# Handing the first token tile from mixer to attention: dealt by transfers and turned by VectorE instead of transposed by TensorE

## The chip, the cores and the metric

The kernel runs on one core of one Trainium2 chip. The metric is the device time of one execution in microseconds (us), as the median of several runs. The engines are TensorE (PE; its weight loads are PEld), VectorE (DVE), ScalarE (ACT), GpSimd (POOL) and SyncE (SP, which here only issues transfers).

## The reference

The model has two layers (DEPTH = 2) on 256 tokens of width 1024, all in float32. Each layer has four steps, and each step ends in a layer norm over the 1024 columns:

```python
h = layer_norm(ALPHA * h + 0.5 * swiglu(h, ffn1...), ln_g[l, 0], ln_b[l, 0])
...   # mixer: z = h @ w_in[l], a gated convolution, a gated recurrence, a multi-scale pooling
h = layer_norm(ALPHA * h + mix, ln_g[l, 1], ln_b[l, 1])          # mix = [...] @ w_out[l]
h = layer_norm(ALPHA * h + cross_attn(h, mem, ca_q[l], ca_k[l], ca_v[l], ca_o[l]), ln_g[l, 2], ln_b[l, 2])
h = layer_norm(ALPHA * h + 0.5 * swiglu(h, ffn2...), ln_g[l, 3], ln_b[l, 3])
```

Cross-attention projects h to queries (ca_q) and a memory of 256 rows to keys and values (ca_k, ca_v), takes a softmax for four heads of width 256, and projects back with ca_o. The change lies between the second and the third line: the norm that ends the mixer, and the way its result reaches the query projection.

## The kernel before, in words

**Split products.** To keep float32 accuracy, every operand of a product is split into a rounded part and a low part (the difference to the rounded part). The helper `split` does it: ScalarE rounds (line 75), VectorE subtracts (line 76). A product is then three matmuls: rounded by rounded, rounded by low, low by rounded (line 132 issues each). Weights arrive through SP's queue in pieces of 128x1024 (`raw`, six places) and are split into `whi` and `wlo` (eight places each). So VectorE and ScalarE work for every weight piece that TensorE uses.

**Tiles of tokens and the transposed copy.** The activation h lies as two tiles of 128 tokens by 1024 columns, `h[0]` and `h[1]`. Products need it with the columns on the partitions: that is `xT`, with the rounded part `xTh` and the low part `xTl`, in eight chunks k of 128 columns. It is made from h by `transposed`: for each half of the chunks four TensorE transposes into PSUM (line 199), then a split.

**The end of a step.** `project_back` multiplies by the output weights in four slabs of two chunks. Its last three slabs are done per token tile inside `finish`: `tile_done(i)` runs the products of tile i for both halves of 512 columns, adds them to h (line 377), takes the statistics of the norm, and applies the norm in two passes (lines 407 and 412). The statistics come in two forms. With `junk` set, line 377 also sums, VectorE forms the mean (line 387), ScalarE squares all 1024 columns with a sum (line 392), VectorE forms the variance (line 398), GpSimd takes the power -1/2 (line 404). Without `junk`, VectorE uses its statistics instruction (line 383), combines them (lines 402 and 403), and GpSimd takes the power. The mixer's end is the one end in a layer that runs without `junk` in this kernel (the kernel's last norm does too). When the products of tile 1 are under way, `turn_first` transposes tile 0; `finish` returns a function, `pend`, that transposes tile 1 later.

**Attention.** `attention` first multiplies memory by the first half of ca_v (`values(l, 0, ...)`, which does not need h), calling `pend` in the middle of the second tile of memory rows, then projects queries (`query(0)`, `query(1)`), four chunks of 128 columns each. For each chunk, `mm_cols` issues seven products of the rounded weights with both parts of `xT`, eight products of the low weights, and the last rounded product. The four softmax heads follow, whose weights are dealt by transfers and turned by VectorE's 32x32 transposes; that pair of steps is a full transpose of the tile. Query weights are loaded behind the mixer's last norm pass (`normed[-1]`) as far as VectorE's queue is concerned, through `tc.issue_after`.

**What sets the order.** The order of each engine's instructions is fixed when the program is built. A scheduler plays the program against estimated durations; among the instructions that are ready it takes the one earliest in program order, and what isn't ready is passed by others. `tc.issue_after(x)` queues the instructions of a block behind x on x's engine. Some stretches of the mixer have an order written out by hand; the handover to attention has none. On the chip each engine then keeps that order and waits on semaphores.

Of the kernel before, what the change touches and what calls it, by code (L numbers as in the profile page):

```python
# [60 lines left out]
def model(ctx: ExitStack, tc: tile.TileContext, t: dict, out: bass.AP):  # L61
# [7 lines left out]
        return ps.tile(list(shape), F32, tag=tag, name=tag)  # L69


    loads, normed, squared, halfway, lows, turns = [], [], [], [], [], []

    def split(hi, lo, src):
        rounded = nc.scalar.copy(hi, src)  # L75
# [117 lines left out]
    kTh = cst.tile([P, NK, SEQ], F32R, name="kTh")  # L193
    kTl = cst.tile([P, NK, SEQ], F32R, name="kTl")

    def transposed_half(src, i, j, dh, dl, unit=idn, keep=None):
        pt = acc((P, 4, P))
        for k in range(4):
            turns.append(nc.tensor.transpose(pt[:, k, :], src[:, (4 * j + k) * P : (4 * j + k + 1) * P], unit))  # L199
        split(dh[:, 4 * j : 4 * j + 4, tok(i)], dl[:, 4 * j : 4 * j + 4, tok(i)], pt)  # L200
        if keep:
            nc.scalar.copy(keep[j], pt)

    def transposed(src, i, dh, dl, unit=idn, keep=None):
        for j in range(2):
            transposed_half(src, i, j, dh, dl, unit, keep)
            if not j:
                halfway.append(lows[-1])

# [115 lines left out]

    squares = kTh[:, 4:8, :].rearrange("p k c -> p (k c)")

    def finish(mm, y, scale, gb, units, last=False, junk=None, ahead=None, prompt=False):

        g, b = gb
        def later_split(i, j, unit):
            pt = acc((P, 4, P))
            for k in range(4):
                turns.append(nc.tensor.transpose(pt[:, k, :], h[i][:, (4 * j + k) * P : (4 * j + k + 1) * P], unit))
            dh, dl = (x[:, 4 * j : 4 * j + 4, tok(i)] for x in (xTh, xTl))
            nc.scalar.copy(dh, pt)  # L340
            return dh, dl, pt

        def turn_first():
            if prompt:
                held.extend(later_split(0, j, units[0]) for j in range(2))
            else:
                transposed(h[0], 0, xTh, xTl, units[0])

        def low_part(w):
            lows.append(nc.vector.tensor_tensor(w[1], w[2], w[0].bitcast(F32), op=ALU.subtract))  # L350

        held = []

        def tile_done(i):

            st = sm.tile([P, 4, 6], F32, tag="st", name="st")
            pieces, size = [slice(0, 512), slice(512, DM)], 512
            if last and i == NT - 1:

                pieces, size = [slice(0, 512), slice(512, 768), slice(768, DM)], 256  # L360
                c = slice(512, DM)
                v = halves(h[i][:, c])
                with tc.issue_after(lows[-1].ins):
                    nc.vector.scalar_tensor_tensor(v, v, ALPHA / scale, sums(y[i][1]), op0=ALU.mult, op1=ALU.add)
            for c in pieces:
                n = c.start // 512
                v = halves(h[i][:, c])
                if len(pieces) == 3 and n:
                    o = acc((P, 256))
                    mm(i, n, slice(c.start - 512, c.stop - 512), o, None)  # L370
                    nc.vector.tensor_tensor(v, v, sums(o), op=ALU.add)
                else:
                    mm(
                        i, n, slice(0, 512), None,
                        None if last or not i or not n else turn_first,
                    )
                    nc.vector.scalar_tensor_tensor(
                        v, v, ALPHA / scale, sums(y[i][n]), op0=ALU.mult, op1=ALU.add,
                        accum_out=None if junk is None else st[:, n, 0:1],
                    )  # L380
                for d in range(c.start, c.stop, size):
                    if junk is None:
                        nc.vector.bn_stats(st[:, d // size, :], h[i][:, d : d + size])
            mv = sm.tile([P, 2], F32, tag="mv", name="mv")
            rs = sm.tile([P, 1], F32, tag="rs", name="rs")
            if junk is not None:
                mean = nc.vector.tensor_scalar(
                    mv[:, 0:1], st[:, 0, 0:1], st[:, 1, 0:1], -1.0 / DM, op0=ALU.add, op1=ALU.mult
                )
                with ExitStack() as behind:  # L390
                    squared.append(
                        nc.scalar.activation(junk, h[i], AF.Square, bias=mv[:, 0:1], accum_out=mv[:, 1:2])
                    )
                    if prompt:
                        with tc.issue_after(mean.ins):
                            low_part(held.pop(0))
                        behind.enter_context(tc.issue_after(lows[-1].ins))
                    nc.vector.tensor_scalar(
                        rs, mv[:, 1:2], 1.0 / DM, LN_EPS / scale / scale, op0=ALU.mult, op1=ALU.add
                    )  # L400
            else:
                nc.vector.bn_aggr(mv, st[:, 0 : DM // size, :])
                nc.vector.tensor_scalar_add(rs, mv[:, 1:2], LN_EPS / scale / scale)
            nc.gpsimd.tensor_tensor(rs, rs, nhalf[:, 0:1], op=ALU.pow)
            cs = [slice(0, 512), slice(512, DM)]
            for c in cs:
                nc.vector.scalar_tensor_tensor(
                    h[i][:, c], h[i][:, c], mv[:, 0:1], g[:, c],
                    op0=ALU.subtract if junk is None else ALU.add, op1=ALU.mult,
                )  # L410
            for c in pieces:
                normed.append(nc.vector.scalar_tensor_tensor(
                    h[i][:, c], h[i][:, c], rs, b[:, c], op0=ALU.mult, op1=ALU.add
                ))
                if last:
                    e = nc.scalar if c.start == 512 else nc.sync
                    e.dma_start(out[0, tok(i), c], h[i][:, c])

        if ahead is None:
            tile_done(0)  # L420
            tile_done(1)
        else:
            split(*ahead.todo[0])
            if prompt:
                nc.scalar.copy(ahead.todo[1][0], ahead.todo[1][2])
                held.append(ahead.todo[1])
            with tc.issue_after(lows[-1].ins):
                tile_done(0)
            with tc.issue_after(normed[-1].ins):
                if prompt:  # L430
                    split(*ahead.todo[2])
                    split(*ahead.todo[3])
                tile_done(1)
                if not prompt:
                    for x in ahead.todo[1:]:
                        split(*x)
            if prompt:
                with tc.issue_after(normed[-1].ins):
                    low_part(held.pop())
        return lambda keep=None: transposed(h[1], 1, xTh, xTl, units[1], keep)  # L440

    def project_back(slabs, late, gb, scale, unit, between=lambda: None):


        y = [[acc((P, 512), "dn") for _ in range(2)] for _ in range(NT)]
# [24 lines left out]
                for k in range(2):  # L470
                    mm(u, i, k, n)

        return finish(tail, y, scale, gb, (unit, unit), junk=squares if unit is pdn else None)


    def ffn(l, name, n, pend=None, last=False, early=None, started=None, following=None):
# [480 lines left out]
    def mixer(l, fill):  # L957
        w_in = t["w_in"][l]
        with tc.tile_pool(name="mix", bufs=1, reuse_waits="tile") as mp:
# [337 lines left out]
            def slab(a):  # L1297
                return lambda: (load(t["w_out"][l], a, 2, 0, DM), xTh[:, a : a + 2, :], xTl[:, a : a + 2, :])

            return project_back([slab(a) for a in (0, 6, 2, 4)], 3, gb, 1.0, idn)  # L1300


    def attention(l, pend):
        scale = (DM // HEADS) ** -0.5
        with tc.tile_pool(name="att", bufs=1, reuse_waits="tile") as ap:
# [1 line left out]
            qTl = ap.tile([P, NK, SEQ], F32R, name="qTl")  # L1307
            vh = ap.tile([P, NT, DM], F32R, name="vh")
            vl = ap.tile([P, NT, DM], F32R, name="vl")
            es, pr = [None] * HEADS, [None] * HEADS  # L1310

            def query(c, between=None):

                with tc.issue_after(normed[-1].ins):
                    w = load(t["ca_q"][l], 0, NK, c * CHUNK, CHUNK)
                for p in range(2):
                    o = sm.tile([P, 2, SEQ], F32, tag="sums", name="sums", bufs=1)
                    for j in range(2):
                        add(o[:, j, :], mm_cols(w, slice((2 * p + j) * P, (2 * p + j + 1) * P), xT))
                    d = slice(4 * c + 2 * p, 4 * c + 2 * p + 2)  # L1320
                    split(qTh[:, d, :], qTl[:, d, :], o)
                    if between is not None and p == 0:
                        between()
# [28 lines left out]

            def deal(hh):
                e = es[hh]
                x = ap.tile([P, 4, 4, 32], F32, tag="dealt", name="dealt", bufs=2)
                for a in range(4):
                    nc.sync.dma_start(x[a * 32 : a * 32 + 32], e[:, a * P : (a + 1) * P])
                pr[hh] = x
# [17 lines left out]
            def mixed(hh, pT):  # L1376
# [8 lines left out]
                for d in range(2):  # L1385
# [2 lines left out]
                        o[:, d, :].rearrange("p (b r i) -> p i r b", i=2, b=4),  # L1388
                    )

            pT = []
            values(l, 0, vh, vl, {6: pend})
            query(0)
            gb = ln_params(l, 2)
            query(1, lambda: (weights(0), deal(0), weights(1), deal(1)))
# [15 lines left out]
            def slab(a):  # L1411
                return lambda: (load(t["ca_o"][l], a, 2, 0, DM), xTh[:, a : a + 2, :], xTl[:, a : a + 2, :])

            return project_back([slab(a) for a in (0, 2, 4, 6)], 3, gb, 1.0, pdn, others)


    def beginnings(op):
# [43 lines left out]
```

## Time and profile before

| | |
|---|---|
| runs | 1063.53 us median of 3 (1063.38 to 1063.78) |
| profiled execution | 1062.78 us, its span 1061.1 us |
| granted TensorE clock | 0.998 |
| GpSimd's dealing of the small feed-forward chunk | six transfers of 64 KB, 4.2 us to landing |
| transfers | 251.06 MB, mean 237 GB/s |

The span is the time from the first to the last instruction of the profiled execution; the execution's own time adds what lies around it. In the rows of a timeline, the first number is the start in us, the second the length, then engine, line, operation, output<-inputs and shape; "xN" at the end says that N neighbouring instructions are merged in the row, and a bracket gives idle time ahead of it with what ended it. A group's row gives minimum, median and maximum length in ns. Matmuls are pipelined, so their lengths overlap, and the distance between starts is their price.

### The profile page before, as it was taken

Reading aid. Unit: us, or ns where it says so; the run is one execution under the profiler, and the core shown is the slowest. Engines: PE = TensorE matmul, PEld = TensorE weight load, DVE = VectorE, ACT = ScalarE, POOL = GpSimd, SP = SyncE. Lnnn points to the kernel's source line nnn. Section 1 sums busy time; section 2 is a strip of 40 time slices with the busy share of each in tenths; the row PEclk is TensorE's granted clock in tenths of the full one; section 3 lists DMA queues with packets and bytes.
Section 4 is the critical chain, followed back from the end, with each engine's and each line's share of the span. In section 5 each row is a group of like instructions: output and inputs, shape, how many; then the busy total and the mean of one; then the engine's idle time right before and its main releaser. Section 6 shows DMA issues by size and latency. Waiting matters only on the chain.

```text
span 1061.1 us, 16496 instructions
## 1 busy us (share of the span) xinstructions
PE 1051.2 (99%) x6014; PEld 934.8 (88%) x6014; DVE 933.2 (88%) x1246; ACT 662.0 (62%) x909; POOL 94.7 (9%) x128
## 2 busy tenths in 40 slices
PE   9999999999999999999999999999999999999996
PEld 7888888889899888889888888998998998888896
DVE  6998898989988789887898987999899787898787
ACT  6675775676557566655665656666774655675661
POOL 8002001000000001010001001010000000000001
PEclk9999999999999999999999999999999999999999
DMA  9999984854675589988789978866636675799971
GB/s 364 296 320 280 260 272 146 268 166 155 210 271 179 171 281 231 363 192 217 239 305 254 338 224 208 271 233 222 206 122 215 241 243 162 242 303 294 241 194 68
DMA packets 142306, 251.06 MB, mean 237 GB/s; under 512 B 11249, under 2 KB 51985, under 8 KB 142225
## 3 DMA queue, kind: packets, MB, share of 16 engines
q1 hardware_dynamic: 130656, 228.89, 65.0%
q0 software_dynamic: 10992, 19.94, 10.9%
q10 hardware_dynamic: 576, 1.18, 0.3%
q8 instruction: 47, 0.77, 0.3%
q14 instruction: 35, 0.28, 0.1%
HBM read 234.50 MB, written 1.05 MB: 222 GB/s over the span
## 4 chain that ended last, share of the span: by engine, by line
PE 92%; DVE 3%; DMA 2%; issue 2%; ACT 1%; POOL 0%; DVEq 0%; ACTq 0%; POOLq 0%
PE acc L132 61%; PE dn L132 27%; DVE wlo L76 2%; PE acc L199 1%; DMA raw<-in_ffn_gate_dram 1%; DMA raw<-in_ffn_down_dram 1%; ACT whi L75 0%; PE dn L1139 0%; DVE raw L702 0%; PE dn L1213 0%; DMA lng<-in_ln_g_dram 0%; DMA h<-in_x_dram 0%; DVE al L76 0%; PE acc L581 0%; DVE square L531 0%
## 5 line engine op out<-in xcount | busy, mean ns | idle before, releaser
L75 ACT CAST whi<-raw 128x1024 fp32r<-128x1024 f32 (+1 forms) x452 | 456.1, 1042 | 201.2 <-PE dn L132 58.0
L76 DVE TENSOR_TENSOR wlo<-raw,whi 128x1024 fp32r<-128x1024 f32 (+1 forms) x452 | 534.5, 1211 | 53.1 <-ACT whi L75 47.1
L132 PE MATMUL acc<-whi,xT 128*128 128x512 f32 (+1 forms) x1064 | 313.9, 372 | 0.0
L132 PEld LDWEIGHTS acc<-whi,xT 128*128 128x128 f32 x1064 | 199.0, 189 | 26.9 <-DVE xT L76 0.3
L132 PE MATMUL acc<-wlo,xT 128*128 128x512 f32 (+1 forms) x532 | 197.9, 372 | 0.0
L132 PE MATMUL dn<-whi,ah 128*128 128x512 f32 x346 | 131.5, 380 | 0.0
L132 PE MATMUL dn<-wlo,ah 128*128 128x512 f32 x346 | 131.3, 379 | 0.0
L132 PE MATMUL dn<-whi,al 128*128 128x512 f32 x346 | 131.1, 379 | 0.0
L132 PE MATMUL acc<-xT,whi 128*128 128x512 f32 x480 | 117.6, 381 | 0.0
L132 PEld LDWEIGHTS acc<-wlo,xT 128*128 128x128 f32 x532 | 100.6, 189 | 13.4
L132 PEld LDWEIGHTS acc<-xT,whi 128*128 128x128 f32 x480 | 86.8, 190 | 9.8
L132 PE MATMUL dn<-whi,xT 128*128 128x512 f32 x288 | 87.7, 380 | 0.0
L132 PEld LDWEIGHTS dn<-wlo,ah 128*128 128x128 f32 x346 | 65.4, 189 | 9.6 <-DVE wlo L76 0.6
L132 PEld LDWEIGHTS dn<-whi,al 128*128 128x128 f32 x346 | 65.4, 189 | 9.2
L132 PEld LDWEIGHTS dn<-whi,ah 128*128 128x128 f32 x346 | 65.4, 189 | 9.0
L132 PEld LDWEIGHTS acc<-xT,wlo 128*128 128x128 f32 x480 | 62.9, 191 | 3.2
L132 PE MATMUL acc<-xT,wlo 128*128 128x256 f32 x480 | 63.2, 275 | 0.0
L132 PE MATMUL acc<-wlo,kTh 128*128 128x512 f32 (+1 forms) x176 | 61.7, 351 | 0.0
L132 PE MATMUL acc<-whi,kTl 128*128 128x512 f32 (+1 forms) x176 | 61.7, 351 | 0.0
L132 PE MATMUL acc<-whi,kTh 128*128 128x512 f32 (+1 forms) x176 | 61.7, 351 | 0.0
L132 PEld LDWEIGHTS dn<-whi,xT 128*128 128x128 f32 x288 | 54.4, 189 | 7.6
L132 PE MATMUL dn<-wlo,xT 128*128 128x512 f32 x144 | 54.6, 379 | 0.0
(252 smaller groups left out, 1296.8 us busy)
## 6 DMA issues: line engine op xcount, KB each, us to landing
raw<-in_ffn_up_dram SPq DMA_DIRECT2D x88, 512.0 KB, 5.7
raw<-in_ffn_down_dram SPq DMA_DIRECT2D x88, 512.0 KB, 5.6
raw<-in_ffn_gate_dram SPq DMA_DIRECT2D x84, 512.0 KB, 5.6
raw<-in_w_in_dram SPq DMA_DIRECT2D x48, 512.0 KB, 4.8
dealt<-sg SPq DMA_DIRECT2D x80, 128.0 KB, 4.5
raw<-in_ffn_up_dram POOLq DMA_DIRECT2D x19, 512.0 KB, 6.3
raw<-in_ffn_gate_dram POOLq DMA_DIRECT2D x16, 512.0 KB, 9.4
raw<-in_ca_k_dram SPq DMA_DIRECT2D x16, 512.0 KB, 5.2
```

The lines of the kernel that those rows point to most:

```text
L75: rounded = nc.scalar.copy(hi, src)
L76: lows.append(nc.vector.tensor_tensor(lo, src, hi.bitcast(F32), op=ALU.subtract))
L132: turns.append(nc.tensor.matmul(o, w, x, start=start, stop=stop, skip_group_check=more))
L199: turns.append(nc.tensor.transpose(pt[:, k, :], src[:, (4 * j + k) * P : (4 * j + k + 1) * P], unit))
```

## The change

The mixer's end no longer transposes tile 0 on TensorE. Once tile 0 is normed, four transfers from GpSimd's queue deal its 32-row blocks into a tile `dealt` (in a place of the mixer that is free by then). After tile 1's norm VectorE turns that in two instructions of 128x512, into a buffer shared with the norm's scale (`lng`), and the split into `xT` is moved into `values`, ahead of the second tile of memory rows (`first_rows`). This gives the columns in another order over the chunks: chunk k, partition p holds column 8p + k. So tile 1's transposes, which stay on TensorE, read h with a step of eight words (`across`), and the query weights are loaded with their rows in the same order (`load(..., across=True)`). The norm at the mixer's end takes the form with the squares on ScalarE (`junk`, on the mixer's free values tile). The attention weights' two dealing places become the halves of one tile.

```diff
-    def transposed_half(src, i, j, dh, dl, unit=idn, keep=None):
+    def transposed_half(src, i, j, dh, dl, unit=idn, keep=None, across=False):
         pt = acc((P, 4, P))
-        for k in range(4):
-            turns.append(nc.tensor.transpose(pt[:, k, :], src[:, (4 * j + k) * P : (4 * j + k + 1) * P], unit))
+        for k in range(4 * j, 4 * j + 4):
+            x = src.rearrange("p (c k) -> p k c", k=NK)[:, k, :] if across else src[:, k * P : (k + 1) * P]
+            turns.append(nc.tensor.transpose(pt[:, k % 4, :], x, unit))
...
-    def finish(mm, y, scale, gb, units, last=False, junk=None, ahead=None, prompt=False):
+    def finish(mm, y, scale, gb, units, last=False, junk=None, ahead=None, prompt=False, across=None):
...
-                        None if last or not i or not n else turn_first,
+                        None if last or across or not i or not n else turn_first,
...
-        if ahead is None:
+        if across is not None:
+            tile_done(0)
+            x = across()
+            for a in range(4):
+                dealt = nc.gpsimd.dma_start(
+                    x[a * 32 : a * 32 + 32].rearrange("p (b c) -> p b c", b=4), h[0][:, a * 256 : (a + 1) * 256]
+                )
+            with tc.issue_after(dealt.ins):
+                tile_done(1)
+            o = wp.tile([P, DM], F32, tag="lng", name="turned").rearrange("p (k t) -> p k t", k=NK)
+            m = x.rearrange("p (b j k) -> p k b j", b=4, k=NK)
+            with tc.issue_after(normed[-1].ins):
+                for d in (slice(0, 4), slice(4, 8)):
+                    nc.vector.transpose(o[:, d].rearrange("p k (r b) -> p k b r", b=4), m[:, d])
+            firsts.append(o)
+        elif ahead is None:
...
-            return project_back([slab(a) for a in (0, 6, 2, 4)], 3, gb, 1.0, idn)
+            return project_back(
+                [slab(a) for a in (0, 6, 2, 4)], 3, gb, 1.0, idn,
+                junk=v.rearrange("p i c -> p (i c)"),
+                across=lambda: mp.tile([P, DM], F32, tag="q", name="dealt"),
+            )
...
-                    w = load(t["ca_q"][l], 0, NK, c * CHUNK, CHUNK)
+                    w = load(t["ca_q"][l], 0, NK, c * CHUNK, CHUNK, across=True)
...
-                x = ap.tile([P, 4, 4, 32], F32, tag="dealt", name="dealt", bufs=2)
+                if not hh:
+                    two.append(ap.tile([P, 2, 512], F32, tag="dealt", name="dealt", bufs=1))
+                x = two[0][:, hh % 2].rearrange("p (a b c) -> p a b c", a=4, b=4)
...
+            def first_rows():
+                for d in (slice(0, 4), slice(4, 8)):
+                    split(xTh[:, d, tok(0)], xTl[:, d, tok(0)], firsts[-1][:, d])
+
             pT = []
-            values(l, 0, vh, vl, {6: pend})
+            values(l, 0, vh, vl, {4: first_rows, 6: pend})
```

More of the change, by code (lines that the diff above doesn't have):

```diff
@@ L69, in acc @@
         return ps.tile(list(shape), F32, tag=tag, name=tag)
-    loads, normed, squared, halfway, lows, turns = [], [], [], [], [], []
+    loads, normed, squared, halfway, firsts, lows, turns = [], [], [], [], [], [], []
     def split(hi, lo, src):
@@ L202, in transposed_half, with transposed @@
             nc.scalar.copy(keep[j], pt)
-    def transposed(src, i, dh, dl, unit=idn, keep=None):
+    def transposed(src, i, dh, dl, unit=idn, keep=None, across=False):
         for j in range(2):
-            transposed_half(src, i, j, dh, dl, unit, keep)
+            transposed_half(src, i, j, dh, dl, unit, keep, across)
             if not j:
@@ L439, in finish, with project_back @@
                     low_part(held.pop())
-        return lambda keep=None: transposed(h[1], 1, xTh, xTl, units[1], keep)
-    def project_back(slabs, late, gb, scale, unit, between=lambda: None):
+        return lambda keep=None: transposed(h[1], 1, xTh, xTl, units[1], keep, across is not None)
+    def project_back(slabs, late, gb, scale, unit, between=lambda: None, junk=None, across=None):
         y = [[acc((P, 512), "dn") for _ in range(2)] for _ in range(NT)]
@@ L471, in tail @@
                     mm(u, i, k, n)
-        return finish(tail, y, scale, gb, (unit, unit), junk=squares if unit is pdn else None)
+        return finish(tail, y, scale, gb, (unit, unit), junk=junk, across=across)
     def ffn(l, name, n, pend=None, last=False, early=None, started=None, following=None):
@@ L1309, in attention @@
             vl = ap.tile([P, NT, DM], F32R, name="vl")
-            es, pr = [None] * HEADS, [None] * HEADS
+            es, pr, two = [None] * HEADS, [None] * HEADS, []
             def query(c, between=None):
                 with tc.issue_after(normed[-1].ins):
-                    w = load(t["ca_q"][l], 0, NK, c * CHUNK, CHUNK)
+                    w = load(t["ca_q"][l], 0, NK, c * CHUNK, CHUNK, across=True)
                 for p in range(2):
@@ L1412, in slab @@
                 return lambda: (load(t["ca_o"][l], a, 2, 0, DM), xTh[:, a : a + 2, :], xTl[:, a : a + 2, :])
-            return project_back([slab(a) for a in (0, 2, 4, 6)], 3, gb, 1.0, pdn, others)
+            return project_back([slab(a) for a in (0, 2, 4, 6)], 3, gb, 1.0, pdn, others, squares)
     def beginnings(op):
```

## The prediction

> **What bounds the kernel now.** I read the page's shares of busy time first, then the timeline of each engine around the first of the two places where the mixer hands over to attention (layer 0, 280 to 303 us).
>
> ```profile
> span 1061.1 us, 16496 instructions
> PE 1051.2 (99%) x6014; PEld 934.8 (88%) x6014; DVE 933.2 (88%) x1246; ACT 662.0 (62%) x909; POOL 94.7 (9%) x128
> ```
>
> TensorE is busy for 99% of the span; a step off it saves its full length if nothing else makes it wait. Its timeline at the handover (start, length, instruction):
>
> ```profile
> 285.43 0.38 PE L132 MATMUL dn<-whi,xT 128*128 128x512 f32 x1
> 285.64 1.04 PE L199 MATMUL acc<-idn,h 128*128 128x128 f32 x8
> 286.43 0.46 PE L132 MATMUL dn<-whi,xT 128*128 128x512 f32 x1
> 286.73 0.38 PE L132 MATMUL dn<-wlo,xT 128*128 128x512 f32 x1
> ...
> 289.11 0.38 PE L132 MATMUL acc<-whi,mT 128*128 128x512 f32 x1
> ...
> 296.88 1.04 PE L199 MATMUL acc<-idn,h 128*128 128x128 f32 x8
> ...
> 300.34 1.67 PE L132 MATMUL acc<-xT,whi 128*128 128x512 f32 x7
> 301.85 1.05 PE L132 MATMUL acc<-xT,wlo 128*128 128x256 f32 x8
> 302.75 1.89 PE L132 MATMUL acc<-xT,whi 128*128 128x512 f32 x8
> ```
>
> Matmuls start 0.216 us apart (11 from 286.73 to 289.11). The reader is to see that TensorE has no hole here: tail of the output projection, eight transposes of token tile 0, rest of the tail, values from 289.11 with the transposes of tile 1 inside them, queries from 300.34. VectorE, same stretch:
>
> ```profile
> 280.66 0.69 DVE L377 SCALAR_TENSOR_TENSOR h<-h,dn 128x512 f32<-128x512 f32 x1 [1.19 <-PE dn L132]
> 281.38 0.69 DVE L383 BATCH_NORM_STATS2 st<-h 128x6 f32<-128x512 f32 x1
> ...
> 285.07 0.68 DVE L377 SCALAR_TENSOR_TENSOR h<-h,dn 128x512 f32<-128x512 f32 x1
> 285.79 0.70 DVE L383 BATCH_NORM_STATS2 st<-h 128x6 f32<-128x512 f32 x1
> 286.40 2.35 DVE L76 TENSOR_TENSOR wlo<-raw,whi 128x1024 fp32r<-128x1024 f32 x2
> 288.65 1.29 DVE L76 TENSOR_TENSOR xT<-acc,xT 128x512 fp32r<-128x512 f32 x2
> 289.85 0.68 DVE L377 SCALAR_TENSOR_TENSOR h<-h,dn 128x512 f32<-128x512 f32 x1
> ...
> 292.94 1.40 DVE L412 SCALAR_TENSOR_TENSOR h<-h,rs,lnb 128x512 f32<-128x512 f32 x2
> 294.27 2.35 DVE L76 TENSOR_TENSOR wlo<-raw,whi 128x1024 fp32r<-128x1024 f32 x2
> 296.54 0.68 DVE L76 TENSOR_TENSOR vl<-acc,vh 128x512 fp32r<-128x512 f32 x1
> 297.14 2.34 DVE L76 TENSOR_TENSOR wlo<-raw,whi 128x1024 fp32r<-128x1024 f32 x2
> 299.41 1.27 DVE L76 TENSOR_TENSOR xT<-acc,xT 128x512 fp32r<-128x512 f32 x2
> 300.60 2.35 DVE L76 TENSOR_TENSOR wlo<-raw,whi 128x1024 fp32r<-128x1024 f32 x2
> ```
>
> No idle time is marked from 285.07 to 300.60: VectorE is a second full engine here. The low part of tile 1's first half ends at 299.41 + 0.60 = 300.0, 0.3 us before the queries need it at 300.34. The query weights' four low parts (two at 294.27, two at 297.14) are done at 299.4, needed from 301.85: 2.4 us to spare. So whatever is added to VectorE between 285 and 300 is soon felt.
>
> **The change part by part, for one layer.** Layer 1 shows the same pattern, with the same cost, at its own handover, so each sum is doubled:
>
> ```profile
> 808.63 1.04 PE L199 MATMUL acc<-idn,h 128*128 128x128 f32 x8
> ```
>
> *Eight transposes leave TensorE.* From 285.43 to 286.73 lie 1.30 us, of which two slots of 0.216 are matmuls: the eight cost 0.87 us. Two layers: 1.74 us, 0.16% of the span. This is all that the change can gain, since TensorE has no hole to close here. All that follows on TensorE is due 0.87 us earlier: end of the tail at 288.24, queries at 299.47, their low-part products from 300.98.
>
> *Squares on ScalarE.* Existing norms of this form give the prices (groups by line, then rows from the timelines of VectorE and ScalarE in the norm after attention):
>
> ```profile
> L392 ACT ACTIVATE kTh<-h,mv x10: 1143/1150/1167, 167.0 to 890.0; 128x1024 fp32r<-128x1024 f32 x10
> L392 ACT ACTIVATION_READ_ACCUMULATOR kTh<-h,mv x10: 183/188/201, 168.0 to 891.1; 128x1 f32 x10
> ```
>
> ```profile
> 366.42 0.21 DVE L387 TENSOR_SCALAR mv<-st 128x1 f32<-128x1 f32 x1
> ...
> 366.76 1.17 ACT L392 ACTIVATE kTh<-h,mv 128x1024 fp32r<-128x1024 f32 x1
> ...
> 368.81 0.15 DVE L398 TENSOR_SCALAR rs<-mv 128x1 f32<-128x1 f32 x1
> ...
> 370.20 1.41 DVE L412 SCALAR_TENSOR_TENSOR h<-h,rs,lnb 128x512 f32<-128x512 f32 x2
> ```
>
> Mean to square 0.34, square with its read 1.25, then 1.39 from the variance to the last pass. Tile 0: sum at 280.66, mean 281.35, square done 282.94, variance 283.0, last pass 284.4 to 285.7. The chain is thus slower than that of 285.07, by 0.6 us. Tile 1: its first sum starts at 285.7, then the two low parts of the value weights (their rounding on ScalarE starts at 285.19, below, so they can't come sooner), second sum at 288.65, mean 289.25, square done 290.85, last pass 292.3 to 293.6. VectorE saves two statistics passes of 0.69 but stands idle about 1.25 us between variance and last pass, as the query weights are queued behind the norm. ScalarE's casts may hold up the square by one piece:
>
> ```profile
> 285.19 1.99 ACT L75 CAST whi<-raw 128x1024 fp32r<-128x1024 f32 x2 [9.67 <-PE dn L132]
> ...
> 288.05 3.90 ACT L75 CAST whi<-raw 128x1024 fp32r<-128x1024 f32 x4
> ...
> 298.04 1.06 ACT L75 CAST xT<-acc 128x512 fp32r<-128x512 f32 x2
> ```
>
> One piece is 0.95 us, so the norm ends between 293.6 and 294.6; today it ends at 294.27. I take 293.6: the norm's square ranks ahead of the query weights' casts in program order. The two halves of tile 1 (at 298.04) take 0.53 each.
>
> *Dealing.* Four transfers issued by GpSimd, each behind the norm of tile 0. The nearest rows are a dealing of half the size:
>
> ```profile
> L525 POOL DMA_DIRECT2D dealt<-both x6: 706/766/832, 511.4 to 1034.7; - x6
> ...
> dealt<-both POOLq DMA_DIRECT2D x6, 64.0 KB, 4.2
> ```
>
> Issues from 285.0 or 285.7 take 4 x 0.77, so the last starts by 288.0 and lands about 292.2: in time for 293.6, and a transfer up to 1.4 us later is still hidden. GpSimd's next task, the power within the 1.39 of tile 1's norm, comes after 290.9 and finds the issues done.
>
> *Turning on VectorE.* No row has its form: it reads every eighth word and writes every fourth. The bounds:
>
> ```profile
> L1366 DVE STREAM_TRANSPOSE square<-dealt x6: 701/707/712, 329.6 to 861.7; 128x512 f32<-128x512 f32 x6
> L229 DVE STREAM_TRANSPOSE turned<-early x4: 1077/1108/1130, 131.8 to 161.7; 128x512 f32<-128x512 f32 x4
> L1292 DVE STREAM_TRANSPOSE yr<-dealt x4: 1152/1360/1555, 259.5 to 785.5; 128x512 f32<-128x512 f32 x4
> ```
>
> L229 reads every eighth word, L1292 writes every fourth; L1366 is the dense floor. I take 1.3 each, 2.6 for two (1.4 to 3.1). The split of tile 0 moves behind it (two at 0.60) and leaves the place at 288.65.
>
> *The new queue.* From 293.6: turning 2.6, low part of the values 0.6, tile 0's 1.2, four query pieces 4 x 1.13, tile 1's 1.2: all done at 303.7 (303.1 to 304.7) instead of 300.6, while TensorE comes 0.87 earlier. Which is late depends on the order. By program order tile 1's split ranks ahead of the query pieces and its rounded half is there at 298.04 + 0.53 - 0.87 = 297.7; with one query piece already begun, it is done at 293.6 + 2.6 + 0.6 + 1.2 + 1.13 + 0.6 = 299.7: TensorE waits 0.2 (0 to 1.3). Query pieces two to four come at 301.4, 302.6 and 303.7; they are wanted from 301.2 to 301.65 (eight low-part products take 0.90, from 301.85 to 302.75). TensorE has cover: the rounded-part products of the other three columns, 3 x 7 x 0.216 = 4.5 us, if the scheduler puts them forward. Then the layer gives -0.87 + 0.2 = -0.67, both -1.3.
>
> *Tile 1's transposes read with a stride.* The eight at 296.88 load every eighth word of h as weights. No row shows such a load. L229's extra over L1366 is 0.40 us for 512 words, 0.1 for 128; eight give 0.8 us a layer. The near row on the engine itself is that matmuls run 0.216 us apart although the helper at L132 feeds them in alternating halves, so I take 0 and keep 0.8. The Trainium skill speaks against the change here: SBUF — State Buffer, "Door 1: The DMA port swizzle", says that consecutive accesses within one 16-byte line run at full rate and each step to a new line is penalised. L229 against L1366 agrees with it on VectorE; no run here shows it for a weight load, and by it the 1.3 us gain would turn into a loss of 0.3.
>
> *At no cost.* The query weights' row order changes which rows a transfer takes, not its size. The loading of the next norm's parameters now waits for tile 0's split, as both use one buffer:
>
> ```profile
> 293.05 0.34 SPq L321 DMA_DIRECT2D lng<-in_ln_g_dram  x1
> ```
>
> It goes from 293.05 to about 297.5, and the last query transfers behind it with it, some 3 us; they serve the fifth column, 10 us after 300.34, so ScalarE and VectorE have room.
>
> **The rivals.**
> 1. TensorE keeps program order. Then the fourth query piece, at 303.7 for 301.65, stops it 2.05 us: +1.2 a layer, +2.4 in all (+1.2 to +4.4 with the ends 303.1 and 304.7). For it: in every row above TensorE goes in program order. Against: so far nothing made it wait, so the rows can't show whether it would be reordered. It decides where the backlog ends after 302.5.
> 2. VectorE keeps today's order, tile 1's split last (at 297.14 the pieces go first): the queries start at 303.1, not 299.47, -0.87 + 3.6 = +2.8 a layer, +5.5. Against: the rounded half would now be there before the second piece.
> 3. The strided load costs its 0.8: -1.3 + 1.6 = +0.3, no change.
> 4. The full gain, -1.74, or a little more by shifts elsewhere.
>
> **How the numbers follow.** The profiled execution took 1062.78 us, its span 1061.1; the median is 0.75 above it. My sum gives 1061.5 against 1062.78, so 1062.2 against the median of 1063.53. Chances: forecast 0.45, strided load 0.12, TensorE in order 0.33, VectorE in today's order 0.08, full gain and shifts beyond it 0.02. A measurement of this kernel can tell about 0.2%, 2.1 us. Faster than that needs more than the whole gain of 1.74: 0.05, from rival 4 and a little of the forecast. The forecast, the strided load and the milder third of rival 1 lie within: 0.62. The rest of rival 1 and rival 2 are slower: 0.33. The range goes from near the full gain, 1061.5 (0.04 below it), to the upper part of rival 1, 1066.8; the rest of rival 1 and rival 2, at 1069.0, make up 0.16 above it.
>
> **What would show it.** Right: no L199 group in the tail, queries reaching TensorE near 299.7, product groups of several columns ahead of the first low-part products, turning at 1.1 to 1.5 us. Wrong: a hole of over 1 us before or inside the first query column, tile 1's weight loads longer than those of today's transposes, the turning held by a transfer.

## The result, and the profile after

| | before | after |
|---|---|---|
| median of 20 runs each, us | 1063.59 (1063.04 to 1065.0) | 1065.28 (1064.44 to 1066.7) |
| ratio after to before | | 1.0016 (95%: 1.0009 to 1.0023) |
| profiled execution, its span, us | 1062.78, 1061.1 | 1064.91, 1063.2 |
| granted TensorE clock | 0.998 | 0.999 |

The kernel became slower by 1.7 us, 0.16%, where a gain of 1.3 us was forecast. The time lies inside the stated range, on the other side of no change. The page of after, its shares of busy time:

```profile
span 1063.2 us, 16487 instructions
PE 1050.1 (99%) x5998; PEld 932.8 (88%) x5998; DVE 932.6 (88%) x1250; ACT 666.8 (63%) x917; POOL 99.6 (9%) x136
```

TensorE has 16 instructions fewer and is busy for 1.1 us less, and yet the span is 2.1 us longer: the transposes are gone and something now makes TensorE stand still. TensorE's timeline at layer 0's handover in after (start, length, instruction; the bracket is idle time before it and what ended it):

```profile
288.23 0.38 PE L132 MATMUL dn<-whi,xT 128*128 128x512 f32 x1
288.44 0.38 PE L132 MATMUL acc<-whi,mT 128*128 128x512 f32 x1
...
296.22 1.04 PE L200 MATMUL acc<-idn,h 128*128 128x128 f32 x8
...
299.47 0.38 PE L132 MATMUL acc<-whi,mT 128*128 128x512 f32 x1
301.47 1.78 PE L132 MATMUL acc<-xT,whi 128*128 128x512 f32 x7 [1.62 <-DVE xT L76]
303.08 0.83 PE L132 MATMUL acc<-xT,wlo 128*128 128x256 f32 x6
303.75 1.25 PE L132 MATMUL acc<-xT,whi 128*128 128x512 f32 x5
...
305.34 0.81 PE L132 MATMUL acc<-xT,whi 128*128 128x512 f32 x3
```

The tail runs into the values without a transpose, as meant. But the queries, which could start 0.22 us after 299.47, start at 301.47: TensorE waits 1.78 us for the low part of tile 1 (`xT`, line 76). Behind that the order is new: rounded-part products of other columns come between the low-part products, at 303.75 and 305.34. VectorE in the same stretch of after:

```profile
291.42 0.15 DVE L399 TENSOR_SCALAR rs<-mv 128x1 f32<-128x1 f32 x1 [1.71 <-ACT v L393]
...
294.13 2.70 DVE L433 STREAM_TRANSPOSE turned<-dealt 128x512 f32<-128x512 f32 x2
296.64 1.24 DVE L76 TENSOR_TENSOR wlo<-raw,whi 128x1024 fp32r<-128x1024 f32 x1
297.78 0.70 DVE L76 TENSOR_TENSOR vl<-acc,vh 128x512 fp32r<-128x512 f32 x1
298.37 1.30 DVE L76 TENSOR_TENSOR xT<-turned,xT 128x512 fp32r<-128x512 f32 x2
299.56 1.25 DVE L76 TENSOR_TENSOR wlo<-raw,whi 128x1024 fp32r<-128x1024 f32 x1
300.69 1.32 DVE L76 TENSOR_TENSOR xT<-acc,xT 128x512 fp32r<-128x512 f32 x2
```

From 294.13 VectorE never rests: turning, one query piece, the values' low part, tile 0's split, a second query piece, and only then tile 1's split, whose first half is done near 301.3. The other new thing is the idle 1.71 us at 291.42, in which VectorE waits for ScalarE's squares. ScalarE in after shows why they are late:

```profile
285.41 4.83 ACT L75 CAST whi<-raw 128x1024 fp32r<-128x1024 f32 x5 [2.31 <-PE dn L132]
290.15 1.15 ACT L393 ACTIVATE v<-h,mv 128x1024 f32<-128x1024 f32 x1
...
297.39 1.99 ACT L75 CAST whi<-raw 128x1024 fp32r<-128x1024 f32 x2
299.28 1.06 ACT L75 CAST xT<-acc 128x512 fp32r<-128x512 f32 x2
```

The square of tile 1 starts at 290.15, behind the last of five casts. Two more casts, of the second query half, hold up tile 1's rounded part until 299.28.

To compare kernels I use two stretches of TensorE in each layer: from the first product of the tail (267.51 before, 267.73 after) to the first query product, and from there to the first product of the scores (316.06 before, 317.58 after). Layer 0, us, all from TensorE's timelines:

| kernel | tail start to queries | queries to scores | sum |
|---|---|---|---|
| before | 32.83 | 15.72 | 48.55 |
| after | 33.74 | 16.11 | 49.85 |
| before less the transposes' 0.87 | 31.96 | 15.72 | 47.68 |

After is 1.78 us behind that last row in the first stretch and 0.39 us in the second. Layer 1 agrees (49.92 against 48.55), so the two handovers lose 2.67 us. The span differs by 2.1 and the medians by 1.7, so some of it comes back elsewhere. A part does in the two feed-forwards that follow layer 0's attention: the transposes that start at 371.75 before start at 373.27 in after, 1.52 us later, and those of 538.65 at 539.80, 1.15 later. Neither trace records a wait of TensorE in between, so how the time comes back is open; no run was spent on it, and the variants below too come out 0.3 to 1.1 us lower in their medians than their two stages say, all but `in_order`.

### The profile page after: what moved, and what is told of

It is laid out like the page before. It is cut to its first block, busy times and chain, and to the rows that moved or that the text cites. A ratio compares the mean times of both kernels' runs of the same rounds, so it can differ in the third digit from the quotient of the medians.

```text
span 1063.2 us, 16487 instructions
## 1 busy us (share of the span) xinstructions
PE 1050.1 (99%) x5998; PEld 932.8 (88%) x5998; DVE 932.6 (88%) x1250; ACT 666.8 (63%) x917; POOL 99.6 (9%) x136
## 4 chain that ended last, share of the span: by engine, by line
PE 92%; DVE 4%; DMA 1%; issue 1%; ACT 1%; POOL 0%; DVEq 0%; ACTq 0%; POOLq 0%; SPq 0%
PE acc L132 61%; PE dn L132 28%; DVE wlo L76 2%; ACT whi L75 1%; PE acc L200 1%; DMA h<-in_x_dram 1%; DMA dealt<-h 1%; DVE turned L433 0%; PE dn L1155 0%; DMA raw<-in_ca_q_dram 0%; PE dn L1229 0%; DVE h L413 0%; DVE raw L718 0%; DVE h L408 0%; DVE al L76 0%
```

## The experiments

Four theories stood against each other. A: VectorE's queue behind tile 1's norm (the turning, and the order of what follows) makes TensorE wait. B: the strided loads of the transposes, or the rows' order of the query weights, cost the time. C: the squares on ScalarE cost it. D: it is VectorE's total work, in whatever order. All edits are made to the kernel after, and each time is the median of the variant beside that of the kernel before on the same chip. Stages are those of the table above, layer 0; layer 1 differs by at most 0.07 us.

**Only the squares** (`squares_only`): no dealing, both tiles transposed on TensorE as before.

```diff
-                across=lambda: mp.tile([P, DM], F32, tag="q", name="dealt"),
...
-                    w = load(t["ca_q"][l], 0, NK, c * CHUNK, CHUNK, across=True)
+                    w = load(t["ca_q"][l], 0, NK, c * CHUNK, CHUNK)
...
-            values(l, 0, vh, vl, {4: first_rows, 6: pend})
+            values(l, 0, vh, vl, {6: pend})
```

> The mixer's norms square on ScalarE, but tile 0 is transposed by TensorE as before; query weights in the old order. Theory A (VectorE's queue after tile 1's norm is what lets TensorE wait): the norm of tile 1 ends 0.3 to 1 us later than 294.27 because the square waits behind casts; tile 1's split has 0.3 us to spare, so the queries start up to 0.7 us late in each layer: 0 to +1.4 us against before. Theory B (the strided weight loads and the query weights' new row order cost): 0. Theory C (the squares alone carry the loss): +1.7 us, the queries about 1.8 us late.

Measured 1063.54 against 1063.52, ratio 1.0003 (0.9994 to 1.0012). The stage is 33.25 + 15.82 = 49.07, 0.52 longer a layer, of which the time shows nothing. After misses its best case by 2.17 us a layer (49.85 against 47.68). So C does not carry the loss, though by the stage the squares may have a part in it.

**Dealing without the squares** (`deal_only`): the call of the mixer's end loses its `junk`, so its norms use VectorE's statistics instruction again.

```diff
-                junk=v.rearrange("p i c -> p (i c)"),
```

> Dealing and turning as in the change, but the mixer's norms keep VectorE's statistics instruction. Theory A: the norm of tile 1 ends about 0.9 us earlier than in the change (293.2), but the queue order now has three query pieces ahead of tile 1's split (turning 2.5, pieces 3.4, values 0.6, tile 0's split 1.2, first half 0.6 after 293.2): the queries start near 301.5 as in the change, time +1 to +2 us against before. Theory B: the same as the change, +1.7. Theory C: no loss, -1.7 to 0 us.

Measured 1069.22 against 1063.52, ratio 1.0054 (1.0041 to 1.0067), far above what any theory gave. The stage is 34.25 + 17.48 = 51.73. VectorE's timeline, then TensorE's, in this kernel:

```profile
293.24 2.96 DVE L433 STREAM_TRANSPOSE turned<-dealt 128x512 f32<-128x512 f32 x2
295.98 1.27 DVE L76 TENSOR_TENSOR wlo<-raw,whi 128x1024 fp32r<-128x1024 f32 x1
...
298.95 2.33 DVE L76 TENSOR_TENSOR wlo<-raw,whi 128x1024 fp32r<-128x1024 f32 x2
301.21 1.27 DVE L76 TENSOR_TENSOR xT<-acc,xT 128x512 fp32r<-128x512 f32 x2
302.41 1.21 DVE L76 TENSOR_TENSOR wlo<-raw,whi 128x1024 fp32r<-128x1024 f32 x1
```

```profile
301.94 2.41 PE L132 MATMUL acc<-xT,whi 128*128 128x512 f32 x7 [2.12 <-DVE xT L76]
304.15 1.91 PE L132 MATMUL acc<-xT,wlo 128*128 128x256 f32 x8
305.86 2.14 PE L132 MATMUL acc<-xT,whi 128*128 128x512 f32 x8
```

Tile 1's norm ends 0.89 us sooner than in after (293.24), and tile 1's split still starts 0.5 us later (301.21), because now three query pieces stand ahead of it. And TensorE is in program order here: seven rounded products, then eight low ones. That was not foreseen: whether the scheduler puts cover forward turns on small shifts.

The order does not explain the second stretch, though. The seven rounded products take 2.21 us from start to start where before has 1.51, the eight low ones 1.71 instead of 0.90, the next eight rounded ones 1.97 instead of 1.72; together that is the 1.76 us by which 17.48 exceeds 15.72. No query piece is late: the fourth is done by 303.6, before the low products start. What differs is the clock that TensorE was granted. A row gives a stretch and its length; busy us and instructions of PE, PEld, DVE, ACT and POOL; then the granted clock, the DMA engines' share and GB/s. First this kernel, then after:

```profile
303.00:306.00 3.00, 3.00 (x13) 2.71 (x12) 2.35 (x3) 0.00 (x0) 0.00 (x0) 0.50 0.94 348
```

```profile
303.00:306.00 3.00, 2.98 (x19) 2.39 (x18) 3.00 (x4) 0.11 (x1) 0.00 (x0) 1.00 0.79 281
```

The clock is 0.50 from about 302.9 to 306.3, and again from about 828.6 to 832.0 in layer 1. Without its 1.76 us the stage would be 49.97, beside after's 49.85, and 2 x 1.76 off the 5.7 us leaves an estimated +2.2, just above the +1 to +2 of theory A. The drop came behind a stop of TensorE of 2.12 us; behind the 1.62 of after the clock stayed at 1.00. That the length of the stop decides is not shown.

**Only the stride** (`stride_only`): no dealing, no squares; both tiles are transposed on TensorE from every eighth word, and the query weights keep the new row order.

```diff
-                junk=v.rearrange("p i c -> p (i c)"),
-                across=lambda: mp.tile([P, DM], F32, tag="q", name="dealt"),
+                step=True,
...
-                transposed(h[0], 0, xTh, xTl, units[0])
+                transposed(h[0], 0, xTh, xTl, units[0], None, step)
...
-            values(l, 0, vh, vl, {4: first_rows, 6: pend})
+            values(l, 0, vh, vl, {6: pend})
```

> No dealing, no turning, no squares on ScalarE: both tiles are transposed by TensorE with the eight-word step, query weights in the new row order. Theory A: no difference, within 0.3 us of before; weight loads near 187 ns instead of 140 but eight transposes still 0.87 us. Theory B: +1.7 us or more, since twice as many loads have the step. Theory C: 0.

Measured 1063.10 against 1063.52, ratio 0.9996 (0.9987 to 1.0005); the stage is 32.85 + 15.72 = 48.57, that of before within 0.02. The transposes' line in the trace of this kernel (count; minimum, median, maximum in ns; first and last start), and after it TensorE's timeline at tile 0:

```profile
L200 PEld LDWEIGHTS acc<-pdn,h x48: 139/140/143, 362.2 to 897.6; 128*128 128x128 f32 x48
...
L200 PEld LDWEIGHTS acc<-idn,h x40: 139/188/198, 172.7 to 822.5; 128*128 128x128 f32 x40
```

```profile
287.35 0.38 PE L132 MATMUL dn<-whi,xT 128*128 128x512 f32 x1
287.56 1.04 PE L200 MATMUL acc<-idn,h 128*128 128x128 f32 x8
288.36 0.46 PE L132 MATMUL dn<-whi,xT 128*128 128x512 f32 x1
288.65 0.38 PE L132 MATMUL dn<-wlo,xT 128*128 128x512 f32 x1
```

The strided loads (`idn`, which holds dense ones too) take 188 ns where dense ones take 140, but eight transposes still cost 0.87 us: from 287.35 to 288.65 are 1.30, less two slots of 0.216. B is out.

**No turning** (`no_turning`): VectorE's two transposes are left out; tile 0's columns are then taken untransposed from h, so the values of the output differ, while the transfers still run.

```diff
-                    nc.vector.transpose(o[:, d].rearrange("p k (r b) -> p k b r", b=4), m[:, d])
-            firsts.append(o)
+            firsts.append(h[0].rearrange("p (k t) -> p k t", k=NK))
```

> The change without VectorE's two turning instructions: tile 0's split reads h directly, so the queries of tile 0 are computed from rows that are not transposed (the transfers are still issued, nobody reads them). Theory A: VectorE has 2.5 us less ahead of tile 1's split, TensorE does not wait, the saved 0.87 us a layer shows: -1.4 to -1.8 us against before. Theory B: +1.7 us, as in the change. Theory C: near the change, +1 to +1.7.

Measured 1062.04 against 1063.52, ratio 0.9991 (0.9982 to 1.0000). TensorE's timeline in this kernel:

```profile
299.48 0.38 PE L132 MATMUL acc<-whi,mT 128*128 128x512 f32 x1
299.89 1.78 PE L132 MATMUL acc<-xT,whi 128*128 128x512 f32 x7
301.50 1.05 PE L132 MATMUL acc<-xT,wlo 128*128 128x256 f32 x8
```

Of the wait 0.2 us is left (from 299.48 + 0.216 to 299.89), and the stage is 32.16 + 15.82 = 47.98, 0.3 above the full gain. The edit takes out more than the turning: tile 0's split, which need not wait for it now, stands inside tile 1's norm (at 286.46 and 289.94 on VectorE) instead of behind it, and the norm ends 1.0 us later, at 295.14. With both, TensorE gains 1.87 us a layer (49.85 less 47.98). A holds, as does D so far.

**Tile 1's split first** (`rows_first`): the query pieces are queued behind tile 1's split, on VectorE and (the second half) on ScalarE. `marks` holds the split's last low part and last rounding.

```diff
-                with tc.issue_after(normed[-1].ins):
+                with tc.issue_after(normed[-1].ins), tc.issue_after(marks[c].ins):
...
+            def second_rows():
+                pend()
+                marks.extend((lows[-1], rounds[-1]))
...
-            values(l, 0, vh, vl, {4: first_rows, 6: pend})
+            values(l, 0, vh, vl, {4: first_rows, 6: second_rows})
```

> The change, with the query pieces' low parts queued behind tile 1's split on VectorE, and the casts of the second query half queued behind tile 1's rounding on ScalarE; no work is added or taken away. Theory A (the order of VectorE's queue sets the wait): tile 1's split is done at 298.4 to 299.7 us, the queries start without a wait near 299.7, the four query pieces end at 304.8 and cost 0.3 to 1 us inside the first columns, as TensorE's order now takes other columns' rounded products ahead: -1.2 to +0.3 us against before. If VectorE's total work, not its order, is the limit (theory D), the wait only moves to the pieces: +1 to +2 us, as in the change.

Measured 1064.14 against 1063.60, ratio 1.0006 (0.9997 to 1.0014); the stage is 31.95 + 17.20 = 49.15. TensorE's timeline in this kernel:

```profile
299.94 1.67 PE L133 MATMUL acc<-xT,whi 128*128 128x512 f32 x7
301.46 0.38 PE L133 MATMUL acc<-xT,wlo 128*128 128x256 f32 x2
302.36 0.49 PE L133 MATMUL acc<-xT,wlo 128*128 128x256 f32 x2 [0.52 <-DVE wlo L77]
302.69 1.25 PE L133 MATMUL acc<-xT,whi 128*128 128x512 f32 x5
304.09 0.49 PE L133 MATMUL acc<-xT,wlo 128*128 128x256 f32 x2 [0.16 <-DVE wlo L77]
```

The queries now start without a wait, at the ideal 31.95, so the wait of after was one of order. But the pieces that gave way are late in turn, and TensorE stops inside the column: the loss moves from the first stretch to the second, and most of it stays. The time, 0.5 us above before, lies between what A and D had expected. The order alone does not bring the gain; D has a share.

**The same without the squares** (`rows_first_stats`): as above, and the mixer's end loses its `junk`.

> As the previous one, but with VectorE's statistics instruction in the mixer's norms instead of the squares on ScalarE. The norm of tile 1 then ended at 293.24 us instead of 294.13 where only the dealing was made. Theory A: everything behind it comes 0.9 us earlier, no wait is left: -1.7 to -0.6 us against before. Theory D: +0.5 to +1.5 us.

Measured 1062.67 against 1063.60, ratio 0.9993 (0.9984 to 1.0002); the stage is 31.96 + 16.52 = 48.48. VectorE's timeline in `rows_first`, then in this kernel:

```profile
294.39 2.74 DVE L434 STREAM_TRANSPOSE turned<-dealt 128x512 f32<-128x512 f32 x2
...
299.91 2.40 DVE L77 TENSOR_TENSOR wlo<-raw,whi 128x1024 fp32r<-128x1024 f32 x2
```

```profile
293.49 2.94 DVE L434 STREAM_TRANSPOSE turned<-dealt 128x512 f32<-128x512 f32 x2
...
299.26 2.33 DVE L77 TENSOR_TENSOR wlo<-raw,whi 128x1024 fp32r<-128x1024 f32 x2
```

With the statistics on VectorE its total work is larger, yet the turning starts 0.9 us earlier and the query pieces 0.65 us earlier, for there is no wait for ScalarE's squares. The stage is 0.67 shorter. Against D in its plain form: less work on VectorE was the slower choice.

**TensorE held in program order** (`in_order`): the kernel after, with the products of the first query half kept in the order of the code.

```diff
-            query(0)
+            with tc.manual_schedule(engines={E.PE}):
+                query(0)
```

> The change with TensorE's order in the first query half written out in program order; VectorE's and ScalarE's order is that of the change. It prices the cover of the prediction (other columns' rounded products taken ahead). Theory A: the start of the queries stays where the change has it (33.7 us after the output projection's start), the fourth query piece ends near 304.9 us and stops the first column for about 1.3 us: the query stage takes 0.9 us a layer longer than in the change, time +1 to +2 us against the change, +2.7 to +3.7 against before. If the cover is worth nothing: as the change, +1.7.

Measured 1068.92 against 1063.60, ratio 1.0043 (1.0029 to 1.0058). The stage is 33.76 + 17.34 = 51.10. TensorE's timeline, then its waits in total (us, times, longest):

```profile
301.96 1.78 PE L132 MATMUL acc<-xT,whi 128*128 128x512 f32 x7 [1.63 <-DVE xT L76]
303.57 0.83 PE L132 MATMUL acc<-xT,wlo 128*128 128x256 f32 x6
305.66 0.49 PE L132 MATMUL acc<-xT,wlo 128*128 128x256 f32 x2 [1.25 <-DVE wlo L76]
```

```profile
PE acc L132 <- DVE xT L76: 3.3, 2, 1.6
PE acc L132 <- DVE wlo L76: 2.6, 2, 1.3
```

The first wait is that of after (1.6 a layer); the second, 1.25 for the fourth query piece, is what the scheduler's reordering hides in after. The cover is worth 1.23 us a layer (17.34 less 16.11), where 0.9 was expected; the time, 5.3 us above before, is beyond the +2.7 to +3.7 expected, and the two stages alone give 5.1. The granted clock stays at 1.00 at both handovers, so here the second stretch is longer by a wait.

**The values' low part last as well** (`values_last`): `rows_first_stats`, and the low part of the values' second tile is queued behind the query pieces instead of among them (an instruction of 0.6 us that only the softmax's products need).

```diff
...
+                if not c:
+                    with tc.issue_after(lows[-1].ins):
+                        held.pop()()
...
```

> As the run with the rows first and the statistics instruction, and in addition the low part of the values' second tile is queued behind the four query pieces on VectorE (the values are needed only after the softmax). Theory A: pieces three and four end 0.6 us earlier, the recorded waits of 0.16 us go, and the query stage takes about 16.2 us instead of 16.5: -0.3 us a layer, -1.6 to -0.6 us against before. If the broken runs of products cost by themselves and not the waits: no better than the run without it, -0.9 us.

Measured 1062.57 against 1063.60, ratio 0.9987 (0.9978 to 0.9996): faster than both kernels by the medians, and the only version whose interval lies wholly below 1. The stage is 31.96 + 16.38 = 48.34. `rows_first_stats` had 1062.67; these two are not told apart. Of the 0.87 us saved a layer, 0.21 arrive in the stage (48.55 less 48.34). So the handovers account for 0.4 of the 1.0 us; the rest lies elsewhere in the kernel and is not explained (`stride_only`, whose stage is that of before, was 0.4 us faster too). TensorE's waits in this kernel explain only a part of the rest:

```profile
PE acc L133 <- DVE wlo L77: 0.4, 2, 0.2
```

That is 0.2 a layer, where the expectation had no wait left, and the second stretch is 0.66 longer than before. What remains is not recorded as a wait. TensorE changes between kinds of product more often here, as in this kernel's timeline:

```profile
301.88 0.74 PE L133 MATMUL acc<-xT,wlo 128*128 128x256 f32 x4
302.46 0.60 PE L133 MATMUL acc<-xT,whi 128*128 128x512 f32 x2
303.26 0.49 PE L133 MATMUL acc<-xT,wlo 128*128 128x256 f32 x2 [0.21 <-DVE wlo L77]
303.59 1.03 PE L133 MATMUL acc<-xT,whi 128*128 128x512 f32 x4
```

Four low-part products occupy 0.58 us and two 0.33, start to start, where eight in a row of before occupy 0.90, or 0.11 each: these two broken runs cost about 0.1 us more each. That would account for much of the rest, but it is argued from spacing and no run isolates it.

## Why the prediction was wrong, by its own steps

**The failing step** is the place of tile 1's split in VectorE's queue: "with one query piece already begun", done at 299.7, "TensorE waits 0.2 (0 to 1.3)". Two pieces stood ahead of it, and the half was done near 301.3. The difference of 1.6 us is one more piece (1.13) and a norm that ended at 294.13 instead of 293.6 (0.53, of which 0.22 is only that the whole tail starts later in after, at 267.73), with the turning 0.1 shorter than taken. The working supposed that tile 1's rounded part would be ready at 297.7, so that program order would put the split first. In the trace ScalarE rounds tile 1 only at 299.28, behind two casts of the second query half, as ScalarE's order has them. The same scheduler gave VectorE the second piece, which was ready, at 299.56. I had counted the casts only for the norm's square, and not for the rounding. `rows_first`, which takes both holds away, starts the queries at the ideal 31.95: that this wait was one of order is shown. That ScalarE's two casts were what made the scheduler put the second piece ahead is read from the trace of after; no run moves them alone.

**The norm's end.** The text left 293.6 to 294.6 open and took the lower end, on the reason that the square ranks ahead of the casts. It does in program order, but the casts were ready first, and the square came at 290.15 instead of 289.6 (0.22 of that is again the later start). The text also put VectorE's idle time between the variance and the last pass; it stands between the mean and the variance (the 1.71 us at 291.42), and the first pass of the norm fills the other place. The sum is the same. `rows_first` against `rows_first_stats` prices the squares on ScalarE at this place: 0.67 us a layer. In after itself, with the order free, their removal (`deal_only`) lengthens the first stretch by 0.51, for a third piece now stands ahead of the split, and the second by 1.37, where the granted clock was 0.50. Without the 1.76 us that the clock cost there, it would be worth nothing (49.97 against 49.85): what it gains at the norm, the order takes away.

**The cover.** That TensorE would put products of other columns forward was right, and so rival 1 did not come true in after. `in_order` gives it: a stop of 1.25 us a layer. Rival 1 had worked out a stop of 2.05 (its +1.2 a layer is that less 0.87) for queries that start on time; in `in_order` they start 1.8 us late, so the piece they stop for is nearer. But the forecast let the cover cost nothing, and the second stretch grew by 0.39 us.

**Rival 2**, tile 1's split behind all four query pieces, was given 0.08 and +5.5 us. After is a milder form of it, two pieces instead of four. `deal_only`, with three pieces ahead, measured +5.7, but that it meets the price of the full form is chance: 2 x 1.76 us of it is the clock at 0.50. The forecast treated the order on VectorE as two cases; it was a scale, and each piece on it takes 1.13 us of VectorE's time.

**Right.** The eight transposes gave 0.87 us: in `rows_first` and `values_last` the first stretch is shorter by just that. The dealing is hidden: the chain of after names the last transfer, from 287.64 to its landing at 292.97, but VectorE is in the norm until 294.13 and turns without idle time before it. The turning was taken as 1.3 each, and two take 2.51 us in after (294.13 to 296.64). The strided load (rival 3) costs no time. The Trainium skill (SBUF — State Buffer, "Door 1: The DMA port swizzle") says that each step to a new 16-byte line is penalised. With 187 to 188 ns for a load against 140 the traces agree that there is a penalty, but it hides behind the products and the transposes' pace is unchanged, so here the measurement decides for a price of 0.

**On the whole**, per layer: -0.87 for the transposes, +1.78 for the wait, +0.39 in the queries is +1.30, where the forecast had -0.67. That the time still lies in the stated range is luck: its upper part was drawn for TensorE in program order, which after does not show, and not for this wait. The Trainium skill's advice for a transpose of 128x128 (VectorE: DVE Perf Modes, "Rules for kernel authors") is to use TensorE where the result may land in PSUM. The runs agree with it so far as the plain change goes: 0.87 us on TensorE was replaced by 2.5 us on a VectorE that is 88% busy. They differ only for the version with the order set by hand, which is 0.1% faster than before by the medians.

## What to carry to other kernels

A step moved from a full engine to a nearly full one is paid by what stands in that engine's queue at the moment, so work out which instructions are *ready* when the queue chooses, including those that a third engine must prepare, and not only which comes first in the program. When such a move pays little, try the move together with an explicit order for what the bottleneck needs first: here the order brought +1.7 us down to +0.5, and with the statistics back on VectorE to -0.9 and -1.0, of which the handovers show -0.1 and -0.4. Test parts with the order fixed as well as free, since under a scheduler an edit alone also moves what it did not touch. And where instructions run slower than their pace, look at the granted clock of that stretch before blaming the order.

## What the runs showed of the hardware that was not expected

TensorE's granted clock can fall in mid-kernel: in `deal_only` it was 0.50 for some 3.4 us at each handover, behind stops of 2.12 us in layer 0 and 2.14 in layer 1, and TensorE took 1.71 us for eight products that take 0.90 otherwise. Behind stops of 1.62 to 1.65 us (after and `in_order`, both layers) it stayed at 1.00; what decides was not looked for.

Loading every eighth word as weights makes a load of 128x128 longer (188 ns against 140) without slowing a row of transposes. VectorE's turning is not of one length. In after the two instructions took 2.51 us from the first start to the next instruction, and in the three kernels of dealing with the statistics on VectorE 2.73 to 2.74 (from 293.24 to 295.98 in `deal_only`); the cause was not looked for.
